# Two small edits to a decoder-trunk kernel: where the wide on-chip tiles begin, and the place of one copy in ScalarE's queue

## The chip, the cores and the metric

The kernel runs on one core of a Trainium2 chip. A core has TensorE (matrix products into PSUM), VectorE and ScalarE (elementwise work), GpSimd (elementwise work that reads and writes SBUF only) and SyncE, which here issues nearly all transfers between HBM and SBUF. In profiles they are PE, DVE, ACT, POOL and SP; PEld is the loading of TensorE's weights, which overlaps the products. The engines run side by side, each works through its own queue in order, and semaphores make one wait for another. The metric is the device time of one execution in microseconds (us); lower is better. A change is judged by the medians of several runs.

## The reference

One decoder layer over 256 tokens of width 1024, in float32, with a cross-attention into 256 memory tokens:

```python
h = rms_norm(x, norm_mix_g)
u, q, kc, vc, ks, vs, kw, vw, g_heads, g_conv, g_attn = split(h @ w_in)
conv_out = conv_module(u, ...)          # a*sigmoid(g), 31-tap causal depthwise convolution, layer norm, silu, @ pw
nsa_out  = nsa_attention(q, ..., g_heads)   # sum over 3 branches: sigmoid(gate logits) * branch(compressed, selected, window)
x = x + (sigmoid(g_conv) * conv_out + sigmoid(g_attn) * nsa_out) @ w_out
x = x + cross_attention(rms_norm(x, norm_x_g), mem, xq_w, xkv_w, xo_w)     # 4 heads of 256
x = x + swiglu(rms_norm(x, norm_ffn_g), ffn_in_w, ffn_out_w)               # 2816 wide
return rms_norm(x, final_norm_g)
```

The attention has 16 heads of 64 in 4 groups. The branch gates are 3 x 16 logits per token, `g_heads`. For 256 tokens all blocks are selected and all keys lie inside the window, so the selected and the window branch are full causal attention with a bias.

## The kernel before, in words

**Layout.** Activations stand with features on the 128 partitions: a 1024 x 256 activation is a tile of 128 x 8 x 256 values, 8192 bytes per partition. Fifteen such *wide* slots (tags L0 to L14, and LL of double width) are used again and again by `long`, `longs` and `twin` under other names: h, memory, q, k, v, gates, the convolution's sums `yt`, the residual streams, the feed-forward's hidden values. Smaller tiles (`small`) hold the weights, the convolution's inputs `vt` and products `vw`, softmax rows and statistics. Slots are laid out in the order of their first use, each on a multiple of 32 bytes. The first ones are constants: `eps_t`, 8 bytes, is the last of them at byte 4544 of each partition, so the wide slots begin at byte 4576 and every 8192 (or 16384) bytes behind it. Behind the wide slots stands `roots0`, a tile of 4 bytes, at 127456, and behind it the split weights at 127488. `roots1`, of the same kind, stands near the end. ScalarE writes a square root into each of the two, so that a table of functions is loaded early; nobody reads them.

**Products.** Most products take float32 in two parts: ScalarE copies a weight chunk of 128 x 1024 to a rounded high part (`f_1h` and the like, L177), VectorE subtracts to get the low part (L179), and TensorE adds up high x high, high x low and low x high, in single-pass matmuls whose moving operand has 256 columns (L244). High and low parts rotate through five buffers each. `gemm` uses the weight chunk as the stationary operand and streams the activation out of a wide tile; `gemm_nat` (for v, vs, vw) streams the weight chunk and uses the activation as stationary. q, kc, vc and k0 (`whole`, L274) use full-precision matmuls, two passes each. The feed-forward streams 512 columns (two runs of 256 out of a wide tile, L1045) and then 256 (L1047); its output product `fo` (L1074) streams 512 columns of weights.

**The stages, in order.** k of the memory; u (input of the convolution); kc, vc; q; ks, kw; vs, vw; the gate logits `g_ps` (L596); the attention gate ga in four chunks (`gate`); attention of 8 pairs of heads, with gc and v of the memory as filling work between; pw; wo; cross-attention (xq, xs, xo_ps, xo); feed-forward f and fo; final norm. TensorE's order is fixed by the order of the code and by `in_line`, which holds a product behind the one before.

**The convolution** runs beside all this. Its 31 taps for 8 feature blocks are shared out: VectorE adds some taps by itself (L410); for the others ScalarE multiplies a shifted input by a tap into a product buffer `vw` (L424, two instructions per tap; four buffers), sometimes GpSimd does (L422), and GpSimd adds each product to `yt` (L426). `convolve(n_v, n_g, marks)` issues the next `n_v` steps of VectorE's part and the next `n_g` taps of the other part behind the marked instructions, at a later priority than the code around it. Later the layer norm sums `yt` on GpSimd.

**Around the copy.** The gate logits leave PSUM by a ScalarE copy `sgn` (L600). Behind the first chunk `gate(0)` of ga, TensorE transposes them by `gt_ps` (L652); ScalarE takes the sigmoid `sgt` of it (L654), VectorE reciprocals (L655, L656). The next chunk `gate(1)` stands behind gt_ps in TensorE's queue.

**The pairs of heads.** `scores(hp)` writes scores into PSUM (L718 in the banks "s", L726 in the one bank "s0"). VectorE adds the bias and takes the minimum (L731 out of "s0", L737 out of "s"), ScalarE the exponentials (L749), VectorE the sums and the scaling (L752 to L759). Then TensorE transposes the weights: `turned("b...")` writes pt_b, also into the bank "s0", and `turned("a...")` pt_a. In the code, pt_b of pair 0 comes behind the scores of pair 1.

Of the kernel before, what the change touches and what calls it, by code (L numbers as in the profile page):

```python
# [11 lines left out]
AF = mybir.ActivationFunctionType  # L12
# [3 lines left out]
P = 128  # L16
# [6 lines left out]
TAPS = 31  # L23
# [75 lines left out]
def tile_hybrid_block(  # L99
# [15 lines left out]
    nc = tc.nc  # L115
# [18 lines left out]
    def small(name, shape, dt=F32, tag=None, bufs=1):  # L134
        return sb.tile(shape, dt, tag=tag or name, name=name, bufs=bufs)
# [10 lines left out]
    def aux(name, shape, tag, bufs):  # L146
        return axp.tile(shape, F32, tag=tag, name=name, bufs=bufs)
# [6 lines left out]
    cpt = small("cpt", [P, CP_END])  # L154
    ones = small("ones", [P, P])
    eps_t = small("eps_t", [P, 2])
    nc.vector.memset(ones, 1.0 / D)
    nc.vector.memset(eps_t[:, 0:1], EPS)
    nc.vector.memset(eps_t[:, 1:2], 256.0 * EPS)
    def roots(name):  # L160

        return nc.scalar.activation(small(name, [P, 1]), eps_t[:, 0:1], AF.Sqrt)

    ident = cpt[:, CP_ID:CP_ID + P]
    eps1, eps256 = eps_t[:, 0:1], eps_t[:, 1:2]
# [18 lines left out]
    first, splits = {}, {}  # L184

    def behind(*marks):

        stack = ExitStack()
        for m in marks:
            stack.enter_context(tc.issue_after(m.ins))  # L190
        return stack
# [3 lines left out]
    def ahead(name, slot, pieces=(4, 4)):  # L195

        w = held[name] = long(f"{name}w", slot, (P, NB, 256))
        at = 0
        for n in pieces:
            nc.sync.dma_start(w[:, at:at + n], wst[CHUNK_AT[name]][:, at:at + n])  # L200
            at += n
# [60 lines left out]
    def gemm_nat(name, x):  # L262
        return gemm(name, x, True)
# [92 lines left out]
    nc.sync.dma_start(ppt, pp)  # L356
    for name, slot in (("k2", 12), ("k3", 11), ("u0", 13)):
        ahead(name, slot)
    roots("roots0")

    def kx(j):
        ps = gemm(f"k{j}", mem) if j else whole("k0", mem_t)
# [76 lines left out]
    def convolve(n_v, n_g, *marks):  # L439

        here = tc.cur_priority
        tc.cur_priority = here + 1500
        with behind(*marks):
            for _ in range(n_v):
                next(on_v, None)
            for _ in range(n_g):
                next(on_g, None)
        tc.cur_priority = here

    for j in range(NB):  # L450
        ps = gemm(f"u{j}", h)
        sg = small(f"sg{j}", [P, S], tag="sg", bufs=3)
        act = nc.scalar.activation(sg, ps[:, 1], AF.Sigmoid)
# [45 lines left out]
    for kv, name in enumerate(("kc", "vc")):  # L499
# [5 lines left out]
        act = nc.scalar.activation(kc[64:128, 1::2, 0:S - 1], ps[64:128, :, 1:S], AF.Copy)  # L505
# [47 lines left out]
    for j in range(4):  # L553
        ps = whole(f"q{j}", hf)
        q0, q1 = ([qt[j // 2][:, 4 * (j % 2) + 2 * b + k] for b in range(2)] for k in range(2))
        for b in range(2):
            nc.scalar.activation(q0[b][0:64], ps[0:64, b], AF.Copy, scale=-0.125)
            act = nc.scalar.activation(q1[b][64:128], ps[64:128, b], AF.Copy, scale=-0.125)
# [14 lines left out]
    for br, name in enumerate(("ks", "kw")):  # L573
        ps = gemm(name, h)

        for lo, g in ((0, 0), (64, 1)):
            for to in (lo, 64 - lo):
                act = nc.scalar.activation(kdh[to:to + 64, g::2, br], ps[lo:lo + 64], AF.Copy)
# [7 lines left out]
    for br, name in enumerate(("vs", "vw")):  # L586
        ps = gemm_nat(name, h)
        act = nc.scalar.activation(vst[:, :, br], ps, AF.Copy)
        convolve(2 * TAPS * br, 3 - br, act, splits[name + "_1"][1])
    ng = 3 * HEADS  # L590
    wg = small("wg", [P, NB, 64])
    nc.sync.dma_start(wg, wgn)
# [1 line left out]
    g_ps = aux("g_ps", [P, S], "s0", 1)  # L594
    for kb in range(NB):
        nc.tensor.matmul(g_ps[64 * (kb % 2):64 * (kb % 2) + 64], lhsT=wg[:, kb], rhs=hf[:, kb], start=kb < 2, stop=kb >= NB - 2)  # L596
    sgn = small("sgn", [P, S], tag="sg", bufs=3)
    igd = small("igd", [P, HEADS, 2, 2])
    igc = small("igc", [P, 2, HEADS])
    nc.scalar.activation(sgn, g_ps, AF.Copy)  # L600

# [452 lines left out]
            accs = residual_first()  # L1056

    with tc.issue_after(silu.ins):
        roots("roots1")

    x3 = long("x3", 0, (P, 2, 2, 512))
    junk = long("junk", 9, (P, 2, 2, 512))
# [171 lines left out]
```

## Time and profile before

| | us |
|---|---|
| median of 3 runs (lowest, highest) | 567.52 (566.59, 569.51) |
| the profiled execution | 566.03 |
| its span in the profile | 564.2 |
| TensorE busy in the span | 552.9 |
| VectorE / ScalarE / GpSimd busy | 413.8 / 363.7 / 144.4 |
| mean granted clock of TensorE | 0.996 |

Times in the profile count from the span's start. A timeline row gives start, duration, engine, line, operation, output<-inputs, size, the number of instructions merged into the row, and in brackets the idle time before and what ended it. Rows of the chain of waits give start, duration, what; "x8" is the number of instructions. Consecutive matmuls overlap in their drawn durations, so the pace of a stream is read from its length in the chain divided by its count, or from start to start. A row of the stretches (windows) gives start:end, length, busy time of PE, PEld, DVE, ACT and POOL with their instruction counts, the granted clock of TensorE as a share of full speed, the share of the DMA engines and GB/s. `g_1h<-g` and the like carry names without buffer numbers.

### The profile page before, as it was taken

What the parts mean: (1) busy time and instruction counts of PE and PEld (TensorE: products, weight loads), DVE (VectorE), ACT (ScalarE), POOL (GpSimd) and SP (SyncE); (2) the same over time, 40 slices, a digit from 0 to 9 for tenths busy, and PEclk for the clock granted to TensorE, in tenths of its full rate; (3) what the DMA queues carried; (4) which work ended last, traced back from release to release, by engine and by line L of the source; (5) the groups of instructions that cost most, each with busy time, mean ns of one, the idle gap of its engine ahead of it and who ended that gap; (6) DMA issues with size and microseconds to landing.
All of it is one profiled execution on the core that took longest, in us unless ns stands there. A gap on an engine that the chain in (4) does not pass through costs nothing.

```text
span 564.2 us, 10254 instructions
## 1 busy us (share of the span) xinstructions
PE 552.9 (98%) x3886; PEld 509.5 (90%) x3886; DVE 413.8 (73%) x772; ACT 363.7 (64%) x689; POOL 144.4 (26%) x129
## 2 busy tenths in 40 slices
PE   8999999999979999999999999999999999999995
PEld 7999998899979999889999999988888888888884
DVE  2798985898958898795768667578878787864531
ACT  4677758689866788789646666477565656563421
POOL 0005997999998000300003100140000000000000
PEclk9999999999989999999999999999999999999999
DMA  8938713456455444424555542446465656566612
GB/s 297 406 115 311 299 39 114 129 173 234 135 191 168 157 144 147 135 78 151 173 195 173 183 157 91 150 151 221 162 212 166 208 166 209 160 214 187 187 38 74
DMA packets 29297, 97.30 MB, mean 172 GB/s; under 512 B 3136, under 2 KB 5952, under 8 KB 28992
## 3 DMA queue, kind: packets, MB, share of 16 engines
q1 hardware_dynamic: 28528, 95.34, 51.3%
q10 hardware_dynamic: 720, 1.31, 0.6%
q8 instruction: 30, 0.49, 0.3%
q14 instruction: 19, 0.16, 0.1%
HBM read 95.39 MB, written 1.25 MB: 171 GB/s over the span
## 4 chain that ended last, share of the span: by engine, by line
PE 89%; POOL 7%; DMA 1%; issue 1%; ACT 1%; ACTq 0%; DVE 0%; POOLq 0%
PE ps_f L1045 15%; PE fo L1074 11%; PE ps_u L244 8%; PE ps_f L1047 7%; POOL yt L426 6%; PE ps_pw L244 4%; PE ps_xq L244 4%; PE ps_wo L244 4%; PE ps_gc L244 4%; PE ps_v L244 4%; PE ps_ga L244 3%; PE ps_k L244 3%; PE ps_q L274 3%; PE ps_xo L244 3%; PE ps_xo L1012 2%; DMA mem_t<-in_memt_dram 1%
## 5 line engine op out<-in xcount | busy, mean ns | idle before, releaser
L426 POOL TENSOR_TENSOR yt<-yt,vw 128x512 f32<-128x512 f32 x65 | 100.7, 1550 | 56.2 <-DMA u<-in_wst_dram 47.8
L424 ACT ACTIVATE vw<-vt,ppt 128x256 f32<-128x256 f32 x110 | 48.2, 500 | 15.2 <-POOL yt L426 15.0
L1045 PE MATMUL ps_f<-g,f_1h 128*128 128x512 f32 x176 | 48.8, 397 | 0.0
L1045 PE MATMUL ps_f<-g,f_0h 128*128 128x512 f32 x176 | 48.2, 397 | 0.0
L1116 POOL TENSOR_SCALAR x<-x,rr 128x512 f32<-128x512 f32 x1 | 0.7, 697 | 180.6 <-DVE rr L1086 180.6
L179 DVE TENSOR_TENSOR f_1l<-f,f_1h 128x1024 fp32r<-128x1024 f32 x22 | 26.9, 1224 | 22.8 <-ACT sl L1052 18.6
L410 DVE SCALAR_TENSOR_TENSOR yp<-vt,ppt,yp 128x256 f32<-128x256 f32 x100 | 40.9, 481 | 0.1
L1045 PEld LDWEIGHTS ps_f<-g,f_1h 128*128 128x128 f32 x176 | 32.8, 188 | 7.7
L1045 PEld LDWEIGHTS ps_f<-g,f_0h 128*128 128x128 f32 x176 | 30.1, 189 | 3.8
L1048 ACT ACTIVATE ab<-ps_f 128x256 f32<-128x256 f32 x44 | 16.5, 375 | 26.0 <-PE ps_f L1047 26.0
L749 ACT ACTIVATE p<-p,mins 128x128 f32<-128x128 f32 (+1 forms) x64 | 28.4, 448 | 3.1 <-DVE mins L731 3.1
L1047 PEld LDWEIGHTS ps_f<-g,f_0l 128*128 128x128 f32 x176 | 26.9, 189 | 3.8
L177 ACT ACTIVATE f_1h<-f 128x1024 fp32r<-128x1024 f32 x22 | 23.3, 1058 | 8.6 <-PE ps_f L1045 8.3
L274 PE MATMUL ps_q<-hf,q 128*128 128x256 f32 x128 | 28.5, 381 | 0.0
L1047 PE MATMUL ps_f<-g,f_0l 128*128 128x256 f32 x176 | 28.3, 283 | 0.0
L1047 PE MATMUL ps_f<-g,f_1l 128*128 128x256 f32 x176 | 28.1, 281 | 0.0
L179 DVE TENSOR_TENSOR f_0l<-f,f_0h 128x1024 fp32r<-128x1024 f32 x22 | 27.4, 1245 | 0.0
L274 PEld LDWEIGHTS ps_q<-hf,q 128*128 128x128 f32 x128 | 24.1, 190 | 3.3
L177 ACT ACTIVATE f_0h<-f 128x1024 fp32r<-128x1024 f32 x22 | 23.1, 1051 | 5.6 <-PE ps_xo L1012 4.7
L1047 PEld LDWEIGHTS ps_f<-g,f_1l 128*128 128x128 f32 x176 | 24.0, 188 | 0.0
L1049 DVE TENSOR_TENSOR ab<-ps_f,ab 128x256 f32<-128x256 f32 x44 | 18.4, 421 | 0.7 <-ACT ab L1048 0.6
L922 POOL COPY acc<-s_wo 128x256 f32<-128x256 f32 x1 | 0.7, 655 | 68.0 <-ACT s_wo L915 68.0
(543 smaller groups left out, 1563.8 us busy)
## 6 DMA issues: line engine op xcount, KB each, us to landing
f<-in_wst_dram SPq DMA_DIRECT2D x44, 512.0 KB, 3.7
fo<-in_wfo_dram SPq DMA_DIRECT2D x22, 512.0 KB, 4.2
u<-in_wst_dram SPq DMA_DIRECT2D x14, 512.0 KB, 6.2
q<-in_wst_dram SPq DMA_DIRECT2D x8, 512.0 KB, 5.0
ga<-in_wst_dram SPq DMA_DIRECT2D x8, 512.0 KB, 3.7
gc<-in_wst_dram SPq DMA_DIRECT2D x8, 512.0 KB, 3.9
v<-in_wst_dram SPq DMA_DIRECT2D x8, 512.0 KB, 4.3
pw<-in_wst_dram SPq DMA_DIRECT2D x8, 512.0 KB, 4.6
```

The source lines that it names most:

```text
L177: copies = [nc.scalar.activation(hi[:, at:at + n], w[:, at:at + n], AF.Copy) for at in range(0, shape[1], n)]
L179: low = nc.vector.tensor_tensor(out=lo[:, at:at + n], in0=w[:, at:at + n], in1=f(hi[:, at:at + n]), op=ALU.subtract)
L244: mm = nc.tensor.matmul(ps[:, b], lhsT=lhsT, rhs=rhs, start=row + b + kb == 0, stop=kb == NB - 1 and row == 2 and b == 1)
L274: mm = nc.tensor.matmul(ps[:, b], lhsT=w[:, k, cs], rhs=x[:, kb], start=kb + b == 0, stop=kb == NB - 1 and b == 1)
L410: nc.vector.scalar_tensor_tensor(out=out[:, i] if t == ts[-1] else acc[i], in0=v, scalar=w, in1=acc[i], op0=ALU.mult, op1=ALU.add)
L424: nc.scalar.activation(pr[:, i], v, AF.Identity, scale=w, bias=col(PP_DB, j + i) if t == 0 else 0.0)
L426: nc.gpsimd.tensor_tensor(out=y, in0=y, in1=pr, op=ALU.add)
L749: exp.append(nc.scalar.activation(t, t, AF.Exp, scale=-1.0, bias=mins[:, hd, qb, br:br + 1], accum_out=sums[:, hd, qb, br:br + 1]))
L1045: nc.tensor.matmul(ps, lhsT=hs[kb // 4][0][:, kb % 4, cs], rhs=fg[:, :, kb], start=kb == 0, stop=False)
L1047: nc.tensor.matmul(ps[:, 1], lhsT=hs[kb // 4][1][:, kb % 4, cs], rhs=fg[:, 0, kb], start=False, stop=kb == NB - 1)
L1049: nc.vector.tensor_tensor(out=ab[:, b], in0=ps[:, 1], in1=ab[:, b], op=ALU.add)
L1074: nc.tensor.matmul(accs[c][tb], lhsT=t, rhs=w[:, k], start=False, stop=kb == NF - 1 and t is tl)
```

## The change

The two 4-byte tiles `roots0` and `roots1` become two columns of one 8-byte tile `table`, which is allocated right behind `eps_t`. It stands at byte 4576, and with it the wide slots move by 32 bytes: the first to 4608, every one now on a multiple of 128 bytes (before, 32 short of one). The tiles behind the wide slots, the split weights at 127488 among them, stay where they were; only three of the last statistics tiles move. And the convolution's steps behind the branch `vw` are cut: its call issues no taps of the ScalarE and GpSimd part any more, and two taps are issued by a new call behind the copy `sgn`.

```diff
     eps_t = small("eps_t", [P, 2])
+    table = small("table", [P, 2])
...
-    def roots(name):
+    def roots(at):

-        return nc.scalar.activation(small(name, [P, 1]), eps_t[:, 0:1], AF.Sqrt)
+        return nc.scalar.activation(table[:, at:at + 1], eps_t[:, 0:1], AF.Sqrt)
...
-    roots("roots0")
+    roots(0)
...
     for br, name in enumerate(("vs", "vw")):
         ps = gemm_nat(name, h)
         act = nc.scalar.activation(vst[:, :, br], ps, AF.Copy)
-        convolve(2 * TAPS * br, 3 - br, act, splits[name + "_1"][1])
+        convolve(2 * TAPS * br, 3 - 3 * br, act, splits[name + "_1"][1])
...
-    nc.scalar.activation(sgn, g_ps, AF.Copy)
+    convolve(0, 2, nc.scalar.activation(sgn, g_ps, AF.Copy))
...
-        roots("roots1")
+        roots(1)
```

All line numbers of the changed kernel are higher by one, since `table` adds a line. ScalarE's queue from the last copy of the branch values (`vals<-ps_vw`) on, before; `sgn` is the copy of the gate logits, a `vw` row is the pair of products of one tap:

```order
L588 ACTIVATE vals<-ps_vw 128x2x256
L424 ACTIVATE vw_25_1743<-vt_356,ppt 128x256 x2
L424 ACTIVATE vw_26_1747<-vt_356,ppt 128x256 x2
L600 ACTIVATE sgn<-g_ps 128x256
L424 ACTIVATE vw_27_1925<-vt_356,ppt 128x256 x2
L177 ACTIVATE ga_1h<-ga_1_1982 128x1024
```

and now:

```order
L589 ACTIVATE vals<-ps_vw 128x2x256
L601 ACTIVATE sgn<-g_ps 128x256
L425 ACTIVATE vw_25_1758<-vt_356,ppt 128x256 x2
L425 ACTIVATE vw_26_1762<-vt_356,ppt 128x256 x2
L425 ACTIVATE vw_27_1925<-vt_356,ppt 128x256 x2
L178 ACTIVATE ga_1h<-ga_1_1982 128x1024
```

The copy has passed two taps, four instructions; nothing else moved on ScalarE. On TensorE, where `gt_ps` needs the copy, the order is what it was (now):

```order
L597 MATMUL g_ps<-hf,wg 64x256 x8
L245 MATMUL ps_ga_1769<-hh,ga_0h 128x256 x8
L245 MATMUL ps_ga_1769<-hl,ga_0h 128x256 x8
L245 MATMUL ps_ga_1769<-hh,ga_0l 128x256 x8
L245 MATMUL ps_ga_1769<-hh,ga_1h 128x256 x8
L245 MATMUL ps_ga_1769<-hl,ga_1h 128x256 x8
L245 MATMUL ps_ga_1769<-hh,ga_1l 128x256 x8
L653 MATMUL gt_ps<-cpt,sgn 128x48 x2
L245 MATMUL ps_ga_1841<-hh,ga_0h 128x256 x8
```

Six groups of the first chunk of ga lie between the gate logits and their transpose. The queues of VectorE, GpSimd and SyncE keep their order too.

## The prediction

> **What bounds the kernel now.** I read the page first, then the chain of waits, then the waits of the stretch where TensorE's clock row dips, then that stretch engine by engine.
>
> ```profile
> PE 552.9 (98%) x3886; PEld 509.5 (90%) x3886; DVE 413.8 (73%) x772; ACT 363.7 (64%) x689; POOL 144.4 (26%) x129
> PE 89%; POOL 7%; DMA 1%; issue 1%; ACT 1%; ACTq 0%; DVE 0%; POOLq 0%
> ```
>
> TensorE is busy for nearly the whole span and makes up 89% of the chain; GpSimd's 7% is the only other part worth a look. So a change pays if it shortens what TensorE executes, or if it removes one of the few places where TensorE stands still. After the start there is only one such place. In the answer on waits, in TensorE's timeline and in ScalarE's:
>
> ```profile
> PE gt_ps L652 <- ACT sgn L600: 3.3, 1, 3.3
> ```
> ```profile
> 147.78 1.95 PE L596 MATMUL g_ps<-hf,wg 128*64 128x256 f32 x16
> 154.50 1.10 PE L244 MATMUL ps_ga<-hh,ga_1l 128*128 128x256 f32 x8
> 158.92 0.65 PE L652 MATMUL gt_ps<-cpt,sgn 128*128 128x48 f32 x4 [3.32 <-ACT sgn L600]
> ```
> ```profile
> 153.23 0.58 ACT L588 ACTIVATE vals<-ps_vw 128x512 f32<-128x512 f32 x1
> 155.49 0.91 ACT L424 ACTIVATE vw<-vt,ppt 128x256 f32<-128x256 f32 x2 [1.68 <-POOL yt L426]
> 157.69 0.91 ACT L424 ACTIVATE vw<-vt,ppt 128x256 f32<-128x256 f32 x2 [1.29 <-POOL yt L426]
> 158.51 0.36 ACT L600 ACTIVATE sgn<-g_ps 128x256 f32<-128x256 f32 x1
> ```
>
> g_ps is complete at 149.73. ScalarE reaches its copy only at 158.51, because two pairs of convolution products stand ahead of it in ScalarE's queue, and each pair waits until GpSimd gives a product buffer back. TensorE stands from 155.60 to 158.92. What follows, in stretches (the seventh column of the answer is the granted clock, PEclk):
>
> ```profile
> 155.80:159.90 4.10, 0.98 (x8) 0.98 (x9) 2.94 (x2) 1.78 (x6) 4.02 (x3) 1.00 0.72 232
> 159.90:163.30 3.40, 3.40 (x19) 3.40 (x18) 1.51 (x1) 2.79 (x6) 3.32 (x3) 0.50 0.47 171
> ```
>
> One microsecond after the end of the stall the clock is halved for 3.4 us. So the stall costs 3.3 us of standing and about 3.4 / 2 = 1.7 us of slow running, 5.0 together.
>
> **The change, part one: where the wide tiles begin.** It moves every tile of the fifteen wide slots by 32 bytes, onto multiples of 128; the weight tiles stood on such multiples before. No transfer or instruction is added or removed. The trace of before holds both placements of a matmul's moving operand, in the chain of waits (start, us, what):
>
> ```profile
> 33.84 44.25 PE ps_u L244 x374
> 94.33 6.91 PE ps_q L274 x32
> 211.81 0.86 PE o L782 x4
> 258.06 3.74 PE ps_v L244 x32
> 288.33 17.04 PE ps_wo L244 x144
> 339.37 2.88 PE xo_ps L977 x24
> 392.44 1.86 PE ps_f L1045 x8
> 493.72 1.86 PE ps_f L1045 x8
> 496.52 61.62 PE fo L1074 x264
> ```
>
> ps_u and ps_wo stream 256 columns out of a wide tile (32 bytes off): 44.25 / 374 and 17.04 / 144 are both 118.3 ns. ps_v takes its 256 columns out of a weight tile (on the multiple) with the wide tile as weights: 3.74 / 32 = 116.9. fo streams 512 aligned columns in 61.62 / 264 = 233.4, or 116.7 for 256. xo_ps, with both operands off, takes 120.0. So I put the offset at 1.6 ns for a single-pass matmul of 256 columns, and 3.3 for the 48 of xo_ps. In the feed-forward part eight of 512 columns (two runs of 256) and eight of 256 alternate: from 392.44 to 496.52 are 37 such blocks of 2.813 us; at 116.7 for each 256 a block is 2.801, so 44 blocks save 0.5 us. The full-precision matmuls do not show it: ps_q, moving operand off, 6.91 / 32 = 216 ns; o of L782, moving operand on the multiple, 0.86 / 4 = 215. I take zero for them.
>
> The other engines show nothing either (groups by form; 128x1024 from and into aligned tiles, then with a wide tile):
>
> ```profile
> L177 ACT ACTIVATE f_1h<-f 128x1024 fp32r<-128x1024 f32 x22 | 23.3, 1058 | 8.6 <-PE ps_f L1045 8.3 <-ACT sl L1052 0.2
> L288 ACT ACTIVATE memh<-mem_t 128x1024 fp32r<-128x1024 f32 x2 | 2.1, 1058 | 5.3 <-DMA mem_t<-in_memt_dram 5.3
> L179 DVE TENSOR_TENSOR f_1l<-f,f_1h 128x1024 fp32r<-128x1024 f32 x22 | 26.9, 1224 | 22.8 <-ACT sl L1052 18.6 <-PE ps_f L1047 2.4 <-ACT uh L288 1.2
> L289 DVE TENSOR_TENSOR meml<-mem_t,memh 128x1024 fp32r<-128x1024 f32 x2 | 2.5, 1226 | 9.1 <-ACT memh L288 9.1
> ```
>
> 1058 against 1058 and 1224 against 1226: zero for ScalarE and VectorE. For GpSimd and for the transfers no row separates the two; I take zero.
>
> The Trainium skill's page "SBUF — State Buffer" (Specifications) speaks against part one: it gives lines of 16 bytes, and 32 bytes off is still on such a line, so nothing should be gained. The rows above differ by 1.6 ns; by the page the terms of this part would be zero, which is the first rival below.
>
> How much of it reaches the end? The program has 144 such matmuls for k and 384 for u, 48 each for ks and kw, 192 each for ga, gc, pw, wo, xq and xo. Those ahead of 112 us count: ScalarE's products for GpSimd waited there for q, and GpSimd for them.
>
> ```profile
> 110.84 0.38 ACT L557 ACTIVATE qt<-ps_q 64x256 fp32r<-64x256 f32 x1 [2.99 <-PE ps_q L274]
> 166.83 0.92 ACT L424 ACTIVATE vw<-vt,ppt 128x256 f32<-128x256 f32 x2 [1.98 <-POOL yt L426]
> 167.65 1.04 ACT L177 ACTIVATE ga_1h<-ga 128x1024 fp32r<-128x1024 f32 x1
> 182.30 1.06 ACT L177 ACTIVATE gc_0h<-gc 128x1024 fp32r<-128x1024 f32 x1 [1.45 <-issue]
> ```
> ```profile
> 113.41 2.63 POOL L426 TENSOR_TENSOR yt<-yt,vw 128x512 f32<-128x512 f32 x2 [1.11 <-ACT vw L424]
> ```
>
> GpSimd had 1.11 us to spare, so (144 + 384) x 1.6 = 0.84 us passes on and is carried by its chain of sums up to 167. What ks, kw, ga and gc save in between (480 x 1.6 = 0.77) I count at nothing, because TensorE will wait for others there (part two). pw, wo, xq and xo: 768 x 1.6 = 1.23. xs and xo_ps: 48 x 1.6 + 48 x 3.3 = 0.24. Feed-forward 0.5. Part one is 0.84 + 1.97 = 2.8 us; its lower bound is zero, its upper 2.8 + 0.77 = 3.6.
>
> **Part two: the copy.** sgn now stands right behind vals, so it runs at 153.7 in ScalarE's idle 1.68 us, four microseconds after g_ps is complete. The products behind it were waiting for GpSimd until 155.49 anyway: 0.36 us inside that cover, zero; without the cover it would delay GpSimd by those 0.36. TensorE goes on to gt_ps at 155.6: 3.3 us of stall and 1.7 us of slow clock go, 5.0, the upper bound.
>
> What is late next is VectorE. TensorE's next dependent step is the transpose pt_b. It takes the bank that the scores of the pair after it were written to, and VectorE has to read those first (L731). VectorE, with its idle times, and TensorE:
>
> ```profile
> 168.72 1.32 DVE L179 TENSOR_TENSOR ga_1l<-ga,ga_1h 128x1024 fp32r<-128x1024 f32 x1 [2.40 <-ACT ga_1h L177]
> 175.06 0.88 DVE L676 TENSOR_TENSOR nsc<-cs_ps,nsc 128x256 f32<-128x256 f32 x2 [0.55 <-PE cs_ps L673]
> 176.16 1.83 DVE L179 TENSOR_TENSOR gc_0l<-gc,gc_0h 128x1024 fp32r<-128x1024 f32 x1 [0.22 <-PE ps_ga L244]
> 180.88 1.55 DVE L179 TENSOR_TENSOR gc_1l<-gc,gc_1h 128x1024 fp32r<-128x1024 f32 x1 [0.67 <-ACT gc_1h L177]
> 183.39 1.23 DVE L179 TENSOR_TENSOR gc_0l<-gc,gc_0h 128x1024 fp32r<-128x1024 f32 x1 [0.97 <-ACT gc_0h L177]
> 185.85 0.17 DVE L752 SCALAR_TENSOR_TENSOR sums<-sums,igd 128x8 f32<-128x8 f32 x1 [1.23 <-ACT p L749]
> 193.43 0.28 DVE L731 CUSTOM_DVE_ANT_0 p<-s,nb 128x128 f32<-128x128 f32 x1
> ```
> ```profile
> 181.10 1.11 PE L244 MATMUL ps_ga<-hl,ga_1h 128*128 128x256 f32 x8
> 193.88 0.62 PE L770 MATMUL pt_b<-cpt,p 128*128 128x128 f32 x4
> ```
>
> VectorE ends at 193.71, TensorE begins at 193.88: a margin of 0.17 us. If VectorE does not come earlier, neither does TensorE. VectorE's step at 168.72 hangs on ScalarE's ga_1h (167.65), and that on GpSimd (166.83), which part two does not make faster. From there to 193.71 VectorE idles 0.55 + 0.22 + 0.67 + 0.97 + 1.23 = 3.64 us. The first two were released by TensorE and go. Of 0.97 and 1.23, what came from ScalarE's 1.45 us at 182.30 goes: it waited for a split buffer that TensorE freed at 181.10 + 1.11 = 182.21. The rest, ScalarE's own exponentials, stays. So VectorE gains 0.55 + 0.22 + 1.45 = 2.2 us (bounds: 0.8, if only the two waits on TensorE go; 3.0, if all but 0.67 go). Part two is worth 2.2 and not 5.0, and a stall of about 3 us reappears ahead of pt_b, near 188 to 191. A second half clock may follow it: 0 to 1.7 us. Since VectorE, without idle time there, holds part of TensorE's next 10 us anyway, I take half, 0.8.
>
> The Trainium skill's "TensorE: Matmul & The Clock Gate" (Part 1) says that the clock is halved after an idle window of about 3.4 us whose start is not tied to the kernel. The 0.50 above, behind 3.3 us of standing, agrees. By it the 0.8 would be 0 or 1.7 from one execution to the next.
>
> **Sum.** 2.8 + 2.2 - 0.8 = 4.2 us. The profiled execution took 566.03 us, 1.8 of them around its span of 564.2: 566.03 - 4.2 = 561.8. The runs have a median of 567.52, 1.5 above it; on their scale it is 563.3, and I forecast 563.0, leaning a little to the profiled one.
>
> **Rivals.** *Alignment does nothing to the matmuls.* Against it: two groups at 118.3 and two at 116.7 to 116.9. For it: in the fast groups the operands also change roles, so the cause could be another. Then part two alone: 2.2 - 0.8 = 1.4, or 566.1. *The stall does not come back*, because VectorE's subtractions run quicker once GpSimd and it meet at other moments (1.83 and 1.55 above against 1.23): all of 5.0 and 3.6, or 8.6, 558.9. Against it: the margin of 0.17. *Slower: the half clock returns again and again.* TensorE, now ahead, would stand at the transposes of each pair of heads, and each stop would bring 3.4 us of half clock, 1.7 us. Four such stretches cost 6.8 against 2.8 + 2.2 = 5.0: 1.8 slower, 569.3; it decides from the third on. Against it: from 176 on TensorE never stood in the trace of before, and the clock was 1.00:
>
> ```profile
> 176.00:265.00 89.00, 89.00 (x749) 82.92 (x749) 74.36 (x259) 73.51 (x198) 9.82 (x20) 1.00 0.41 130
> ```
>
> *The change does not do what it says* I rule out: the order and the addresses are in the built program.
>
> **Chances.** Forecast 0.70, alignment void 0.17, no new stall 0.08, slower 0.05. The forecast's own bounds: 2.8 + 3.0 = 5.8 gives 561.7 (560.2 on the profile's scale), 2.8 + 0.8 - 1.7 = 1.9 gives 565.6. The range 560.2 to 566.3 takes in the first rival's centre and leaves out the second and the third. Half a per cent, what a measurement of this kernel can tell from none, is 2.8 us, so faster begins below 564.7. Of the forecast I put 0.63 there, with the second rival 0.71; same 0.24; slower 0.05.
>
> **What would show it.** In the profile of the changed kernel: ps_u and ps_wo at 116.7 ns (118.3 would void part one); sgn right behind vals near 153, with no wait of gt_ps; a wait of pt_b on VectorE's L732 of about 3 us near 190; the clock row with its dip one place later, or none. Wrong would be a time above 566.3, or a pt_b without a wait.

## The result, and the profile after

| | before | changed |
|---|---|---|
| median of six runs (us) | 568.08 | 563.97 |
| ratio, 95% interval | | 0.9931 (0.9905 to 0.9957) |
| profiled execution, its span (us) | 566.03, 564.2 | 563.54, 561.8 |

The gain is 3.9 us (2.4 to 5.4), and 563.97 lies in the range forecast. One execution of the changed kernel took 1939.32 us; it stands in the median of six (563.85 of the five others) and is left out of the ratio. The page and the waits of TensorE in the changed kernel (its lines are the old ones plus one):

```profile
PE 552.1 (98%) x3886; PEld 511.7 (91%) x3886; DVE 415.2 (74%) x772; ACT 362.3 (64%) x689; POOL 145.9 (26%) x129
...
PEclk9999999999999999999999999999999999999999
...
PE 96%; DMA 1%; DVE 1%; ACTq 0%; ACT 0%; issue 0%; DVEq 0%
```
```profile
PE pt_b L771 <- DVE mins L732: 2.0, 1, 2.0
```

GpSimd has left the chain, the clock row has no 8 in it, and the wait of gt_ps is gone from the answer on waits. A wait of pt_b has come, of 2.0 us. TensorE's timeline around both places, and ScalarE's around the copy:

```profile
155.63 1.12 PE L245 MATMUL ps_ga<-hh,ga_1l 128*128 128x256 f32 x8
156.59 0.54 PE L653 MATMUL gt_ps<-cpt,sgn 128*128 128x48 f32 x4
...
192.29 0.63 PE L771 MATMUL pt_b<-cpt,p 128*128 128x128 f32 x4 [1.97 <-DVE mins L732]
```
```profile
153.84 0.57 ACT L589 ACTIVATE vals<-ps_vw 128x512 f32<-128x512 f32 x1
154.32 0.36 ACT L601 ACTIVATE sgn<-g_ps 128x256 f32<-128x256 f32 x1
156.24 0.91 ACT L425 ACTIVATE vw<-vt,ppt 128x256 f32<-128x256 f32 x2 [1.55 <-POOL yt L427]
```

sgn stands right behind vals, gt_ps follows ps_ga without idle time, and the stretches that the prediction quoted are full and at full clock now (the seventh column is the granted clock):

```profile
155.80:159.90 4.10, 4.10 (x37) 4.10 (x37) 3.72 (x2) 1.82 (x4) 3.94 (x3) 1.00 0.64 218
159.90:163.30 3.40, 3.40 (x32) 3.40 (x31) 0.70 (x1) 1.95 (x4) 3.32 (x4) 1.00 0.61 211
```

So far the order of events is as forecast. The chain of waits (start, length, what) is not:

```profile
33.80 44.88 PE ps_u L245 x374
...
94.93 6.91 PE ps_q L275 x32
...
143.16 5.76 PE ps_vw L245 x48
...
264.39 23.21 PE ps_pw L245 x192
287.60 17.28 PE ps_wo L245 x144
...
339.18 2.88 PE xo_ps L978 x24
...
392.50 1.84 PE ps_f L1046 x8
...
493.06 1.84 PE ps_f L1046 x8
495.86 59.88 PE fo L1075 x264
```

ps_u and ps_wo went from 118.3 ns a matmul to 44.88 / 374 = 17.28 / 144 = 120.0, not to 116.7. ps_vw takes 5.76 / 48 = 120.0, where products of its kind (ps_v) took 116.9. fo, which was to stay at 233.4, takes 59.88 / 264 = 226.8. The 37 feed-forward blocks from 392.50 to 495.86 take 2.793 us each (2.813 before). The alignment made the products of 256 columns slower and those of 512 faster. With ps_pw's row in the chain of the kernel before,

```profile
265.41 22.91 PE ps_pw L244 x192
```

pw, wo, xq and xo lose four times 23.21 - 22.91 = 0.30 us, 1.2 in all; fo wins 61.62 - 59.88 = 1.7 and the feed-forward 44 x 0.020 = 0.9. The total came out as forecast, then, with a part one that worked in another way. The experiments had to settle what each part was worth.

### The profile page after: what moved, and what is told of

It reads as the page before. It is cut to its first block, busy times and chain, and to the rows that moved or that the text cites. A ratio compares the mean times of both kernels' runs of the same rounds, so it can differ in the third digit from the quotient of the medians.

```text
span 561.8 us, 10254 instructions
## 1 busy us (share of the span) xinstructions
PE 552.1 (98%) x3886; PEld 511.7 (91%) x3886; DVE 415.2 (74%) x772; ACT 362.3 (64%) x689; POOL 145.9 (26%) x129
## 4 chain that ended last, share of the span: by engine, by line
PE 96%; DMA 1%; DVE 1%; ACTq 0%; ACT 0%; issue 0%; DVEq 0%
PE ps_f L1046 14%; PE fo L1075 11%; PE ps_u L245 8%; PE ps_f L1048 7%; PE ps_q L275 5%; PE ps_ga L245 4%; PE ps_pw L245 4%; PE ps_xq L245 4%; PE ps_wo L245 4%; PE ps_v L245 4%; PE ps_gc L245 3%; PE ps_k L245 3%; PE ps_xo L245 3%; PE ps_xo L1013 2%; DMA mem_t<-in_memt_dram 1%; PE pt_a L771 1%
```

## The experiments

Theory P is the prediction's: a moving operand on a multiple of 128 is faster, and the alignment gains 2.8 us, the copy 1.4. Theory R, formed from the rows above: what counts is how the moving and the stationary operand stand to each other. In the kernel before, the split weights stood 32 bytes further than the wide tiles (modulo 128); in the changed one the distance is 0. xo_ps, with both operands in wide tiles, had the distance 0 in both kernels, and takes 120.0 in both.

For what the clock costs, each execution has a mean granted clock, given in steps of 0.001 (0.6 us). "Lost to the clock" is span x (1 - clock), and "rest" is the time without that. One stretch of 3.4 us at half clock is 1.7 us, or 0.003 of the clock. Not all that is so counted delays anything: in all fourteen profiles the clock also falls to a half at the very end of the span, behind TensorE's last matmul. That is 0.4 to 2.2 us of the amount, 1.4 on average, and no matmul is there to be slowed. In the kernel before, the last matmul ends at 558.1, and behind it (seventh column, the clock):

```profile
561.00:564.00 3.00, 0.00 (x0) 0.00 (x0) 0.00 (x0) 0.00 (x0) 0.00 (x0) 0.78 0.46 170
```

In the profile of the changed kernel all of the 1.1 us lies there. So "lost" is too high and "rest" too low by about that much in every row, and it is differences between rows that are read below. Means over the executions of each kernel:

| | weights from wide tiles, bytes | median us | lost to the clock | rest | wait of TensorE (profile) |
|---|---|---|---|---|---|
| before (17 executions beside the first four experiments) | 32 | 567.48 | 4.5 | 563.0 | gt_ps 3.3 |
| changed (1.1 and 563.1 of the five) | 0 | 563.97 | 1.1 | 563.1 | pt_b 2.0 |
| copy alone | 32 | 563.96 | 2.1 | 562.2 | pt_b 2.5 |
| alignment alone | 0 | 568.07 | 4.5 | 563.4 | gt_ps 2.9 |
| changed, 32 bytes between | 32 | 564.89 | 2.5 | 562.0 | pt_b 2.4 |
| changed, 64 between | 64 | 556.87 | 2.4 | 554.6 | pt_b 3.1 |
| changed, 96 between | 96 | 564.16 | 2.2 | 562.0 | pt_b 2.1 |
| changed, 128 between | 128 | 564.87 | 2.3 | 562.6 | pt_b 2.3 |
| changed, 256 between | 256 | 563.44 | 1.2 | 562.1 | pt_b 1.7 |
| copy, old wide tiles, 64 | 64 | 557.63 | 3.1 | 554.4 | pt_b 2.9 |
| 64, softmax later | 64 | 560.30 | 3.5 | 557.0 | pt_b 0.7, pc_ps 3.2 |
| changed, softmax later | 0 | 567.17 | 2.8 | 564.1 | pc_ps 2.9 |
| 64, values earlier | 64 | 555.69 | 1.9 | 554.2 | pt_b 2.6 |
| copy, values earlier | 32 | 563.80 | 2.1 | 561.8 | pt_b 2.0 |

### Each part alone

The copy alone is the kernel before with these lines:

```diff
-        convolve(2 * TAPS * br, 3 - br, act, splits[name + "_1"][1])
+        convolve(2 * TAPS * br, 3 - 3 * br, act, splits[name + "_1"][1])
...
-    nc.scalar.activation(sgn, g_ps, AF.Copy)
+    convolve(0, 2, nc.scalar.activation(sgn, g_ps, AF.Copy))
```

> The kernel before with the copy's move alone; the wide tiles stay 32 bytes off. Prediction's account: the copy is worth 1.4 us, so 566.7 beside 568.1 for the kernel before, gemm matmuls at 118.3 ns. New account (relative placement: a single-pass matmul of 256 columns takes 120.0 ns when moving and stationary operand start on the same offset modulo 64, 116.7 to 118.3 when they differ; fo's 512 columns take 226.8 instead of 233.3 when they are the same): TensorE gets to pt_b earlier, VectorE does not, so the wait of pt_b is about 3 us instead of 2.0; behind it pw, wo, xq, xo gain 768 x 1.7 = 1.3 us against the changed kernel and fo and the feed-forward lose 1.7 + 0.9 = 2.6: about 564.5 (563.5 to 565.5), within 1 us of the changed kernel.

The alignment alone is the change without them, with `table` and `roots(at)`.

> The kernel before with the wide tiles moved onto multiples of 128 alone; the copy stays behind the four products. Prediction's account: 2.8 us less than the kernel before, 565.3. New account: gemm at 120.0, fo at 226.8; about 1 us is lost ahead of the stall at gt_ps and taken out of that stall, 1.3 is lost behind it and 2.6 won in the feed-forward: 566.5 to 568, at most 1.5 us below the kernel before, with the stall of gt_ps and perhaps the half clock as before.

The copy alone: 563.96 us, ratio 0.9943 (0.9926 to 0.996), 3.2 us (2.3 to 4.2) below the kernel before and on the changed kernel's median. The alignment alone: 568.07, ratio 1.0011 (0.9993 to 1.0029), between 0.4 us won and 1.6 lost, so no difference is shown. As far as the runs can tell, the whole gain is the copy's. Waits of the copy alone, then of the alignment alone, with the stretch behind its wait:

```profile
PE pt_b L770 <- DVE mins L731: 2.5, 1, 2.5
```
```profile
PE gt_ps L653 <- ACT sgn L601: 2.9, 1, 2.9
```
```profile
160.20:163.60 3.40, 3.40 (x19) 3.40 (x19) 1.12 (x1) 2.40 (x5) 3.32 (x4) 0.53 0.52 176
```

With the alignment alone TensorE waits 0.4 us less at gt_ps because it comes later, and the half clock stands behind it as before. By the table the copy's gain consists of 0.8 us of rest (a stall of 3.3 became one of 2.5) and 2.4 us of clock. The kernel before lost 4.5 us to the clock on the average of its executions, where its profiled one lost 2.5 on the same scale: a single stretch of 1.7 behind gt_ps and 0.8 behind the last matmul. Its 17 executions run from 565.89 us at a clock of 0.995 to 569.16 at 0.989, so most of their spread is the clock too.

### The distance between weights and wide tiles

The wide tiles stay where the change put them. A tile behind them pushes the split weights on, and a second one, written once by GpSimd, brings what follows back onto the same multiples of 128 (here 32 + 96 bytes):

```diff
     def roots(at):
-
-        return nc.scalar.activation(table[:, at:at + 1], eps_t[:, 0:1], AF.Sqrt)
+        to = table if at else small("roots0", [P, 8])
+        return nc.scalar.activation(to[:, at:at + 1], eps_t[:, 0:1], AF.Sqrt)
...
+        if name == "1":
+            nc.gpsimd.memset(small("pad", [P, 24]), 0.0)
         r = small(f"r_{name}", [P, 2], tag="rnat", bufs=2)
```

> The changed kernel with 32 bytes between the wide tiles and the split weights: wide tiles on multiples of 128 as changed, split weights at 32 modulo 64, everything behind them on the same multiples of 128 as before. Relative placement: gemm's pairs are now 0 and 32 and take 116.7 ns (118.3 at most) instead of 120.0, fo's pairs differ too and it goes back from 226.8 to about 233.3; 3.3 x 768 = 2.5 us are won behind pt_b, about 1 of what is won ahead of it passes, 1.7 to 2.6 are lost in fo and the feed-forward: 561.5 to 563.5. Rival, the place of the wide tiles themselves decides (a multiple of 128 is the slow place): the wide tiles do not move here, gemm stays at 120.0, and the time stays within 0.5 us of the changed kernel.

> The same with 64 bytes: wide tiles at 0, split weights at 64 modulo 128. If 64 bytes is the period, this is the changed kernel again: gemm 120.0, fo 226.8, time within 0.5 us of it. If 128 bytes is the period, it behaves like the kernel with 32 bytes: gemm 116.7 to 118.3.

With 32 bytes (chain of waits):

```profile
33.94 44.26 PE ps_u L245 x374
...
287.47 17.04 PE ps_wo L245 x144
...
495.62 61.62 PE fo L1077 x264
```

118.3 for ps_u and ps_wo and 233.4 for fo: the kernel before again, though the wide tiles stand on multiples of 128. So the wide tiles' own place is not what counts, and the rival falls; that gemm would reach 116.7 was wrong. The median is 564.89, outside the 561.5 to 563.5 expected: gemm gained 1.7 ns a matmul against the changed kernel and not 3.3, and 2.5 us were lost to the clock where the changed kernel lost 1.1.

With 64 bytes:

```profile
33.50 42.39 PE ps_u L245 x374
...
128.74 5.66 PE ps_kw L245 x48
...
282.84 16.32 PE ps_wo L245 x144
...
487.31 60.44 PE fo L1077 x264
```

42.39 / 374 = 16.32 / 144 = 113.3 ns, faster than either case expected; fo 228.9. ps_kw, a gemm of the same placement, takes 5.66 / 48 = 117.9: at this distance there are two paces, each steady over long stretches, and what picks one is not shown. 556.87 us, ratio 0.9815 (0.9791 to 0.9838), 10.5 us below the kernel before. Both periods named in the expectation, 64 and 128, left a case out: it behaves neither like 0 nor like 32. Hence the next experiments (roots0 of 32, 64 and 24 columns, pad of 32, 32 and 8), and one in which the wide tiles stand where they stood before the change:

> The changed kernel with 128 bytes between the wide tiles and the split weights (the tiles behind stay on the same multiples of 128). If what counts is the distance of the weights from the wide tiles modulo 128, this is the changed kernel again: ps_u and ps_wo at 120.0 ns, fo at 226.8, about 564.0 us. If the period is longer than 128, gemm is faster than that, 113.3 to 118, and the time 556 to 563.

> The same with 256 bytes. Period 128 or 256: 120.0 ns, fo at 226.8, about 564.0 us. A longer period: faster than that, 113.3 to 118 ns.

> The same with 96 bytes: the weights stand 32 short of the next multiple of 128. If the distance modulo 128 counts, and its sign with it, gemm now has the distance that ps_v had in the kernel before (116.7 ns) and ps_v the one that gemm had there (118.3): 1.6 ns less than with 32 bytes for 1776 matmuls and 1.6 more for 288, behind pt_b 768 x 1.6 = 1.2 us: 563.0 to 564.5. If only equal or unequal counts: as with 32 bytes, 118.3 and 564.9.

> The copy's move as changed, but the wide tiles where they stood in the kernel before (32 short of a multiple of 128), and the split weights moved by 32, so that they are 64 apart modulo 128. If only the distance counts: as the kernel with 64 bytes, ps_u, ps_pw and ps_wo at 113.3 ns and 555.5 to 558.7 us. Rival, the wide tiles also have to stand on a multiple of 64: ps_u at 116 or more, 561 us or more.

For the last one, on the copy alone:

```diff
-        return nc.scalar.activation(small(name, [P, 1]), eps_t[:, 0:1], AF.Sqrt)
+        return nc.scalar.activation(small(name, [P, 16])[:, 0:1], eps_t[:, 0:1], AF.Sqrt)
...
+        if name == "1":
+            nc.gpsimd.memset(small("pad", [P, 24]), 0.0)
```

Chains of waits with 128, with 256, with 96, and of the old wide tiles with 64:

```profile
34.11 44.38 PE ps_u L245 x374
...
496.55 61.36 PE fo L1077 x264
```
```profile
33.73 44.88 PE ps_u L245 x374
...
495.47 59.88 PE fo L1077 x264
```
```profile
34.47 44.38 PE ps_u L245 x374
...
131.82 5.76 PE ps_kw L245 x48
...
286.99 16.90 PE ps_wo L245 x144
...
494.55 61.61 PE fo L1077 x264
```
```profile
33.48 42.39 PE ps_u L244 x374
...
487.05 60.44 PE fo L1076 x264
```

128 bytes are not 0 (118.7 and 232.4), 256 are (120.0 and 226.8, to the last digit): 128 is no period, and 256 behaves as one. The old wide tiles with 64 bytes give the same 42.39 and 60.44 as the new ones, and 557.63 us, ratio 0.9829 (0.9783 to 0.9876). So theory R stands in this form: the distance counts, not the place. It is not all that counts: like 64 bytes, 96 bytes have more than one pace in a run, 118.7 for ps_u, 120.0 for ps_kw and 117.4 for ps_wo. The 116.7 expected there was not seen; fo takes 233.4. Why a distance is fast or slow is not shown by these runs. The Trainium skill's "SBUF — State Buffer" (SBUF: two separate sides) says that TensorE never waits on anyone. These rows don't show a wait for another engine, for the distance is one between TensorE's own two operands; but by that statement alone the 113.3 and the 120.0 would not differ.

### VectorE's queue ahead of pt_b, and the clock

The prediction put the returning stall down to VectorE. In front of the minima of pair 1 stand 2.64 us of the compressed branch's softmax and of its products into the values. The first attempt issues all of it behind those minima:

```diff
-    compressed_weights(*exp[-2:])
...
+        reds.append(red)
         return p0, p1
...
                 weights(hp + 1, *p[hp + 1])
+            if hp == 0:
+                compressed_weights(*copies[-3:], reds[1])
```

> The kernel with 64 bytes, and the softmax of the compressed branch (three of its VectorE groups, 0.68 + 1.28 + 0.68 = 2.64 us, stood in VectorE's queue ahead of the minima of pair 1 that pt_b waits for) issued behind those minima. If VectorE's queue is what brings the stall back, the wait of pt_b shrinks from 3.1 to about 0.5 us. Over the executions the kernel with 64 bytes took 554.6 us besides what the lowered clock cost it, and that cost 2.4 us on average; if the clock is lowered because TensorE stands there, that goes back to about 1.1 as well: 552.0 + 1.1 = 553 (552 to 554.5). If the lowered clock has nothing to do with this stall: 552.0 + 2.4 = 554.4. Rival, the stall only moves on to the next pair, because VectorE has the same work to do by then: 556 to 557.

> The changed kernel with the same step behind the minima of pair 1; its wait of pt_b is 2.0 us and its average cost of the lowered clock 1.1 us already. VectorE's queue as cause: the wait goes, 564.0 - 2.0 = 562.0, the cost of the clock stays near 1.1. If the stall only moves on: 564.0.

Waits and two stretches of the kernel with 64 bytes, and VectorE's timeline ahead of the new wait:

```profile
PE pc_ps L874 <- DVE nsc L700: 3.2, 1, 3.2
...
PE pt_b L776 <- DVE mins L736: 0.7, 1, 0.7
```
```profile
202.10:205.30 3.20, 0.04 (x1) 0.00 (x0) 3.20 (x7) 1.55 (x4) 0.00 (x0) 0.82 0.76 213
205.30:211.00 5.70, 5.65 (x23) 5.30 (x24) 4.05 (x24) 2.95 (x12) 0.00 (x0) 0.50 0.36 114
```
```profile
199.41 1.22 DVE L180 TENSOR_TENSOR v_1l<-v,v_1h 128x1024 fp32r<-128x1024 f32 x1
...
200.83 2.46 DVE L625 TENSOR_TENSOR yt<-yt,mu 128x512 f32<-128x512 f32 x4
...
203.42 1.18 DVE L180 TENSOR_TENSOR v_0l<-v,v_0h 128x1024 fp32r<-128x1024 f32 x1
204.51 0.69 DVE L700 TENSOR_TENSOR nsc<-nsc,sumc 128x512 f32<-128x512 f32 x1
```

The wait of pt_b fell to 0.7, as VectorE's queue as cause demands. But the softmax now stands behind v's subtractions and the layer norm, and the next step that needs it, the transpose pc_ps, waits 3.2 us. Two half-clock stretches in a row begin in that wait: the clock is halved from 204.1, 2.0 us after the matmul before had ended, to 210.9. 560.30 us, ratio 0.9879 (0.9849 to 0.9908), against 556.87 and 0.9815; on the changed kernel 567.17, ratio 0.999 (0.9974 to 1.0007), against 563.97 and 0.9931 (pc_ps 2.9, pt_b without a wait). The rival that the stall moves on took both, and at a higher price than it had named.

The second attempt moves only the two products into the values, which hang on nothing late, into a gap of 3.07 us that VectorE had near 160:

```diff
     mark = gate(2, few)
+    hm = cpt[:, CP_HM:CP_HM + 8].unsqueeze(2).to_broadcast([P, 8, HD])
+    with behind(splits["ga2_1"][1]):
+        for i in range(2):
+            nc.vector.tensor_tensor(out=vcm[:, 8 * i:8 * i + 8], in0=vcs[:, i].unsqueeze(1).to_broadcast([P, 8, HD]),
+                                    in1=hm, op=ALU.mult)
```

with the same lines taken out of `compressed_weights`.

> The kernel with 64 bytes, and of the compressed branch only the two products into the values (1.28 us, which hang on nothing late) moved up in VectorE's queue into the 3.07 us that VectorE stood ahead of ga_0l near 160; the softmax itself stays where it was. If VectorE's queue ahead of the minima is the cause, the wait of pt_b goes from 3.1 to 1.8 us and nothing appears at pc_ps. Time without the lowered clock 554.6 - 1.3 = 553.3. If the clock falls because of the length of this stall (1.1 us lost on average at a stall of 2.0, 2.1 to 2.5 at 2.6 to 3.2), 1.1 comes on top: 554.4. If the lowered clock does not depend on it: 553.3 + 2.4 = 555.7. Rival, the stall moves on: 556.5 to 557.

> The kernel before with the copy's move and the same step of the two products; tiles as before. The copy alone left a wait of pt_b of 2.6 us, 562.2 us besides the lowered clock and 2.1 us lost to it. VectorE's queue as cause: wait 1.3, 560.9 besides the clock; with a stall that short 1.1 or less lost, 562.0 in all; if the lost clock does not depend on the stall, 563.0. Rival, the stall moves on: 564.0.

555.69 us, ratio 0.9794 (0.9767 to 0.9821), and 563.80 for the copy with them. The waits fell by about half a microsecond, from 3.1 to 2.6 and from 2.5 to 2.0, not by the 1.28 moved. The groups of the two products, where they stood (64 bytes) and where they stand now, and GpSimd's row beside the latter:

```profile
L702 DVE TENSOR_TENSOR vals<-vcs,cpt x2: 680/682/683, 184.1 to 184.7; 128x512 f32<-128x512 f32 x2
```
```profile
L689 DVE TENSOR_TENSOR vals<-vcs,cpt x2: 1762/1770/1777, 161.0 to 162.7; 128x512 f32<-128x512 f32 x2
```

```profile
158.74 5.20 POOL L429 TENSOR_TENSOR yt<-yt,vw 128x512 f32<-128x512 f32 x3
```

At 184 GpSimd is idle; at 161 it adds the convolution's products, and each of the two takes 1770 ns instead of 682. They no longer fit the gap, and ga_0l starts at 164.42 instead of 162.87. The Trainium skill's "SBUF — State Buffer" (SBUF: two separate sides) has a port pair that VectorE and GpSimd share and hold for a whole instruction; the two durations agree with it. Of the versions run, this one has the lowest median; its interval overlaps that of the 64 bytes alone, so the step itself is not shown to gain.

On the clock: in all fourteen profiles a half clock of 3.4 us (once two in a row) begins within 1.4 us of the end of a wait of TensorE, and nowhere else before the last matmul: behind gt_ps (waits of 3.3 and 2.9), at pc_ps (3.2 and 2.9), where it begins 2.0 and 2.2 us into the wait, and behind pt_b with 32 bytes (2.4) and with 128 (2.3). That of 32 bytes:

```profile
191.60:195.00 3.40, 3.40 (x19) 3.40 (x19) 3.33 (x12) 3.40 (x14) 0.00 (x0) 0.55 0.57 206
```

It does not come each time: the profiles with waits of pt_b of 3.1, 2.9, 2.6 and 2.5 have none, and none has come behind a wait of 2.1 or less. The averages lost go with it only roughly: 1.1 and 1.2 us at waits of 2.0 and 1.7 (distance 0 and 256), but 2.1 also with the copy and the values at 2.0. So in these profiles no half clock came without a stall; that the stall's length alone sets the loss is not shown, nor where the executions without a profile lost theirs. The Trainium skill's "TensorE: Matmul & The Clock Gate" (Part 1) names an idle window of about 3.4 us; half clocks behind waits of 2.3 and 2.4 us, and 2.0 us into one, are outside that, and the numbers measured here decide.

## Why the prediction was right

The total was right: 4.2 us forecast, 3.9 measured, but as the sum of two terms that were both wrong and made up for each other; that the total came out so close was luck.

- **Part one, 2.8 us, failed.** Measured alone it shows no gain (ratio 1.0011, 0.9993 to 1.0029). The step that failed is "I put the offset at 1.6 ns": it read the difference between ps_u and ps_v as one of the moving operand's place, though the two also change roles. The runs show the distance of the two operands in its place: 32 bytes 118.3, 0 bytes 120.0, 64 bytes 113.3 or 117.9. The row that told it was quoted: xo_ps, at 120.0, both of whose operands stand in wide tiles, at distance 0. The change brought every gemm to that distance. I read that row as "both off" and charged it to the offset as well.
- **fo unchanged** was wrong (233.4 to 226.8), and **0.5 for the feed-forward** was 0.9; these 2.6 us won about cover the 256-column products' loss behind pt_b (1.2 for pw, wo, xq and xo, and ps_v's). Zero for the two-pass products held: ps_q's 32 matmuls take 6.91 us in both kernels.
- **The rival "alignment does nothing"** had the right time for part one, and for a wrong reason: the matmuls did change, in both directions. The Trainium skill's "SBUF — State Buffer" (Specifications), cited there, has lines of 16 bytes; distances of 0, 32 and 64 bytes are all multiples of that, and 120.0, 118.3 and 113.3 differ all the same.
- **Part two's mechanism held**: sgn behind vals (154.32), no wait of gt_ps, a new wait of pt_b on VectorE's minima. The size of the stall was 2.5 us at the old pace of TensorE (forecast about 3) and 2.0 in the changed kernel, whose TensorE comes later.
- **Part two's size, 2.2 less 0.8, was too small by more than half**: 3.2 us measured for the copy alone. The 2.2 held: between the two profiled executions pt_b starts 2.2 us earlier (191.67 for 193.88), and the times are 566.03 and 563.88. Two steps failed, both on the clock. The 0.8 given back for a second half clock: the profile of the copy alone has none before the last matmul, and over the executions the clock gained 2.4 us. And the price of the clock from the one profiled execution: that one lost 2.5 us where the executions lost 4.5 on average. Taking the sum on that execution's scale hid it; its time of 566.03 stood 1.5 us under the median shown, and that was the sign.
- **The slower rival**, half clocks at each new stop, did not come in the changed kernel, but what it described is what happened when the softmax was put later: a stop of 3.2 us in which two half clocks in a row began.

## What to carry to other kernels

A row that shows two things changed at once (here the place of an operand and its role) prices neither; look for the row that already has the combination that the edit will produce. Before moving tiles to a round address, measure the distance between the tiles that one matmul reads: a distance of 64 bytes was worth about 7 us (ratio 0.9815 with the copy, 0.9943 for the copy alone) where the multiple of 128 was worth nothing. And price a stall of TensorE over the clocks of several executions, not from the one in the profile, and leave out the lowered clock behind the last matmul.

## What was not expected of the hardware

- Back-to-back single-pass matmuls of 256 columns, weights out of a split tile and columns out of a wide one, take 120.0 ns at a distance (as in the table above) of 0 or 256 bytes, 118.3 at 32, 113.3 or 117.9 at 64, 117.4 to 120.0 at 96 and 118.7 at 128. With the roles exchanged, 32 bytes gave 116.9 (ps_v).
- fo, 512 columns with the roles exchanged, takes 226.8 (0, 256), 228.9 (64), 232.4 (128) or 233.4 (32, 96). The order is not that of the 256 columns: distance 0 is the worst for those and the best for fo.
- A half clock of 3.4 us came behind waits as short as 2.3 us and 2.0 us into a longer one, not at each wait.
- A VectorE product of two SBUF operands took 682 ns beside an idle GpSimd and 1770 beside a busy one.
